# Partial sums of the down products parked in HBM, a ring of five places for second tiles, and two more units of seven products

## The chip, the core and the metric

The kernel runs on one core of a Trainium2 chip. TensorE (PE) multiplies, VectorE (DVE) and ScalarE (ACT) work elementwise, GpSimd (POOL) and SyncE (SP) are used here to issue DMA transfers. Each engine takes its instructions from a queue of its own, in order; an instruction that waits holds up all that stand behind it. The metric is the device time of one execution in microseconds (us).

## The reference

One encoder layer on 256 tokens of width 2048, in float32: a mixing sub-layer (attention and a recurrent block, `w_in`, `w_out`), a SwiGLU channel sub-layer with an inner width of 5632, and a per-layer embedding. The change lies in the middle one and its seams:

```python
h = h + rms_norm(mixed, g_mix_post[i])
fn = rms_norm(h, g_ffn_pre[i])
ff = (jax.nn.silu(fn @ w_ffn_gate[i]) * (fn @ w_ffn_up[i])) @ w_ffn_down[i]
h = h + rms_norm(ff, g_ffn_post[i])
gate = jax.nn.sigmoid(rms_norm(h, g_ple_pre[i]) @ w_ple_gate[i])
ple = p[i] @ w_ple_proj[i]
h = h + rms_norm(gate * ple, g_ple_post[i])
```

## The kernel before

**Products.** Every float32 operand is split in two parts of a narrower type: a cast on ScalarE gives the high part (`wh`, L614), a subtraction on VectorE the low part (`wl`, L627). A product is three matmuls, high x high, low x high, high x low (L661 to L663 in `products`, L672 to L674 in `product`). A weight tile is 256 rows by 512 columns, 512 KB, loaded by SyncE (L522 in the channel sub-layer, L539 elsewhere) into one of four places `wr` or a fifth, `third`. It serves 2 blocks of rows x 2 halves of the tokens x 3 = 12 matmuls of 512 columns.

**The channel sub-layer** goes in three parts of the inner width, `PARTS`: column chunks f = 0 to 3, 4 to 7, 8 to 10 of 512. In each part a group multiplies the gate and up tiles of one f in turns; their product goes to `mid`, is transposed (L333, and 16 small transfers `mT<-mid`, L343, on POOL and SyncE) and split again. Then two groups multiply the part with `w_ffn_down`, output chunks 0 and 1, and 2 and 3. The sums over the parts stand in `mg`: part 0 is copied there by ScalarE (L1778), part 1 added by VectorE (L1781), part 2 added in `Sub.chunk` (L1466), which also squares and multiplies with the gain (L1478).

**Units of seven.** Two tiles of the same rows (gate and up, or two down chunks), two blocks of rows and two halves of the tokens are a 2 x 2 x 2 product of blocks, eight products. A unit does it in seven, 21 matmuls instead of 24, with sums of blocks. `SEVEN_KS` names the blocks of rows treated so in the gate and up groups from f = 2 on (three units each), `DOWN_KS` those of the down groups of parts 0 and 1 (two units each). The host exchanges halves of the two tiles for it. For a unit, `sum_stream` adds weights on VectorE (L562, L566, L572), a third block comes from HBM by a transfer that adds to what is there (`added`, L583, POOL's queue). The unit then has a segment of four products in the group before its own (`four_products`), one of two (`two_products`) and a share in one of one (`one_product`); `made_of_four` combines the sums in PSUM. `issue` mixes these segments with the ordinary tiles of the group, by the tables `TAKEN` and `SPREAD`. The needed differences of activations are made by `sums_of`, `third_sums` (for `hF`) and `mid_sums` (for `mid`).

**Places.** The second tile R of a unit is held from its load until the split for its two products. It has three places, one for each number of the unit in its group: two in `lower`, which lies where the first half of the residual `h` was, and one in a half of `ple`. `h` and the other half of `ple` are written to HBM for the time of the channel sub-layer (`spill_h`, `spill_half`), and come back near its end (`reload_h`, L1596; `reload_half`, L1614). `pTh` and `pTl`, the split embedding input, are overwritten by the third sums, so `load_pT` (L1410) loads and splits `pT` a second time. The gain's tile serves as a fifth place for split weights until the last unit is through; then the gain `g_ffn_post` is loaded (L1422).

**The order** on the queues is decided when the program is built, by the class `Plan`: each piece of work is a generator that asks for an engine, a cost and perhaps a place; the planner starts whatever can start soonest by its own costs, and instructions are put on the queues in that order. `plan.add(work, ready, late)` hands it a piece with the time before which it isn't to start and a bonus or handicap. So a load that is handed over at `plan.clk["pe"]` is issued as soon as SyncE reaches it.

Of the kernel before, what the change touches and what calls it, by code (L numbers as in the profile page):

```python
# [39 lines left out]
DOWN_KS = (0, 2)  # L40
# [6 lines left out]
        (lambda c: (("w_ffn_down", c), ("w_ffn_down", c + 1)), (0, 2), [4 * f0 + k for k in DOWN_KS])  # L47
        for f0, _ in SEVEN_PARTS
# [186 lines left out]
def layer(ctx: ExitStack, tc: tile.TileContext, a: dict, out: bass.AP):  # L235
# [5 lines left out]
    plan = Plan(wr=R_BUFS, w=W_BUFS, sm=SM_BUFS, acc=4, ev=1, mid=2, bt=2, m2=1, mt=1, sq=1, T0=1, T1=1, T4=1, **{f"{s}{j}": n for s, m, n in (("p", 3, 1), ("t", 3, 0)) for j in range(m)}, wr0=1, w0=1)  # L241
# [188 lines left out]
    class Group:  # L430
# [23 lines left out]
        def two(self, j):  # L454
# [3 lines left out]
            lower[self.own[j] + 1] = j  # L458
# [13 lines left out]
        def issue(self, nxt):  # L472
# [7 lines left out]
            more = [lambda j=j: self.two(j) for j in range(len(self.sevens))]  # L480
            if self.sevens:
                more += [lambda js=js: self.one(js) for js in (range(2), range(2, len(self.sevens))) if js]
            for i, k in enumerate(self.rest[:m]):
                for j in range(len(nxt.sevens) if nxt else 0):
                    if i == n - 1 - (SPREAD if n > 5 and len(nxt.sevens) < 3 else 1) * (len(nxt.sevens) - 1 - j):
                        nxt.four(j)
# [3 lines left out]
                for _ in range(TAKEN.get((len(self.sevens), n), ())[i : i + 1][0] if more else 0):  # L490
                    more.pop(0)()
# [3 lines left out]
    SPREAD = 2  # L495
    TAKEN = {(2, 6): (1, 1, 1), (3, 5): (2, 3), (2, 4): (1, 2)}
# [14 lines left out]
    def load_stream():  # L511
        for i, tl in enumerate(tiles):
# [104 lines left out]
    def lo_stream():  # L617
        last_one = max(f[1] for f in fours.values())
        for i in range(len(tiles)):
# [12 lines left out]
            if i == half_end:  # L632
                plan.add(reload_half(), plan.now, -SOON)
# [99 lines left out]
    def two_products(group, j, i):  # L733
# [43 lines left out]
    def third_sums():  # L777
        for e in ev_embedded:
            yield e
        hi, lo = pT_pair()  # L780
        yield from sums_of(hF, 4, *(x.rearrange("p k s -> p (k s)") for x in (hi, lo)))
# [4 lines left out]

    def free_w(i):
# [1358 lines left out]
```

## Time and profile before

| | us |
|---|---|
| median of 3 runs | 1164.94 (1162.43 to 1167.70) |
| the profiled execution, its span | 1163.89, 1162.1 |
| TensorE busy in it | 1148.7 |
| VectorE, ScalarE busy | 883.0, 703.0 |
| bytes read from HBM, written | 242.57 MB, 5.24 MB |

A row of a group of instructions has line, engine, operation, what it writes and reads, count, then busy time and mean duration. A row of the order of time has start, duration, instruction, and in brackets the idle time before it and what ended it. "SPq" is SyncE's queue. `x222` behind a busy time is the number of instructions in the stretch. The channel sub-layer runs from about 350 to 1060 us: the down products of part 0 up to 620, those of part 1 up to 870, those of part 2 from about 988 to 1055.

### The profile page before, as it was taken

How to read it: one execution, taken by the hardware profiler on the slowest of the kernel's cores; microseconds unless marked ns; L12 is line 12 of the kernel's file. 1: busy time of each engine (PE TensorE's matmuls, PEld its weight loads, DVE VectorE, ACT ScalarE, POOL GpSimd, SP SyncE). 2: the span in 40 equal slices, each digit the busy share in tenths (PEclk: the TensorE clock that was granted, in tenths of full speed). 3: DMA queues.
4: the chain of work that ended last, by engine and by line, in shares of the span. 5: the costliest groups of instructions: out<-in, count | busy, mean ns of one | idle time of the engine just before them, and what ended most of it. 6: DMA issues, size and time to landing. Idle time of an engine off the chain costs nothing.

```text
span 1162.1 us, 15025 instructions
## 1 busy us (share of the span) xinstructions
PE 1148.7 (99%) x5225; PEld 951.3 (82%) x5225; DVE 883.0 (76%) x1096; ACT 703.0 (60%) x933; POOL 120.9 (10%) x198
## 2 busy tenths in 40 slices
PE   9999999999999999999999999999999999999997
PEld 7888888888888888788888888888888887887786
DVE  6678787888468777988778888887778884668575
ACT  6777777875456655655546556565455554456564
POOL 0000000000000123031000223312000311100000
PEclk9999999999999999999999999999999999999999
DMA  9867566546676887876775777877667668854772
GB/s 315 288 188 222 185 181 206 175 149 211 228 272 197 291 256 226 261 215 203 252 224 190 249 224 205 263 239 216 207 208 252 205 216 291 249 190 161 216 248 77
DMA packets 109964, 257.21 MB, mean 221 GB/s; under 512 B 38976, under 2 KB 46144, under 8 KB 108736
## 3 DMA queue, kind: packets, MB, share of 16 engines
q1 hardware_dynamic: 99552, 241.73, 62.5%
q0 software_dynamic: 9904, 14.17, 7.4%
q8 instruction: 41, 0.67, 0.2%
q10 hardware_dynamic: 432, 0.35, 0.1%
q14 instruction: 35, 0.29, 0.1%
HBM read 242.57 MB, written 5.24 MB: 213 GB/s over the span
## 4 chain that ended last, share of the span: by engine, by line
PE 86%; DMA 5%; DVE 4%; ACT 2%; issue 1%; POOL 1%; SPq 0%; ACTq 0%; DVEq 0%; POOLq 0%
PE acc L663 23%; PE acc L662 23%; PE acc L661 23%; PE acc L674 4%; PE acc L673 4%; PE acc L672 4%; DMA mT<-mid 3%; DVE wl L627 1%; POOL mT L343 1%; PE tr L324 1%; ACT wh L614 1%; DMA wr<-in_w_ple_gate 1%; DMA pw<-in_pT 1%; PE warm L2055 0%; PE pg L355 0%
## 5 line engine op out<-in xcount | busy, mean ns | idle before, releaser
L627 DVE TENSOR_TENSOR wl<-wr,wh 128x1024 fp32r<-128x1024 f32 (+1 forms) x313 | 373.9, 1209 | 131.7 <-ACT wh L614 129.7
L614 ACT CAST wh<-wr 128x1024 fp32r<-128x1024 f32 (+1 forms) x313 | 323.8, 1043 | 212.0 <-PE acc L662 142.0
L661 PE MATMUL acc<-wh,hT_mix_hi 128*128 128x512 f32 x420 | 164.4, 391 | 2.6 <-ACT wh L614 2.6
L662 PE MATMUL acc<-wh,hT_mix_lo 128*128 128x512 f32 x420 | 164.1, 391 | 0.3 <-DVE hT_mix_lo L313 0.3
L663 PE MATMUL acc<-wl,hT_mix_hi 128*128 128x512 f32 x420 | 164.2, 391 | 0.1
L343 POOL DMA_DIRECT2D mT<-mid x152 | 88.5, 589 | 570.0 <-DMA wr<-in_w_ffn_up 401.9
L663 PE MATMUL acc<-wl,hT_hi 128*128 128x512 f32 x320 | 124.9, 391 | 0.0
L661 PE MATMUL acc<-wh,hT_hi 128*128 128x512 f32 x316 | 124.4, 394 | 0.0
L662 PE MATMUL acc<-wh,hT_lo 128*128 128x512 f32 x316 | 123.1, 390 | 0.0
L661 PEld LDWEIGHTS acc<-wh,hT_mix_hi 128*128 128x128 f32 x420 | 79.2, 189 | 19.3 <-ACT wh L614 3.0
L614 ACT CAST wh<-ple 128x1024 fp32r<-128x1024 f32 (+1 forms) x52 | 51.8, 995 | 70.6 <-DVE ple L566 26.5
L663 PEld LDWEIGHTS acc<-wl,hT_mix_hi 128*128 128x128 f32 x420 | 79.1, 188 | 17.5 <-DVE wl L627 1.3
L662 PEld LDWEIGHTS acc<-wh,hT_mix_lo 128*128 128x128 f32 x420 | 79.2, 189 | 17.3 <-DVE hT_mix_lo L313 1.0
L663 PEld LDWEIGHTS acc<-wl,hT_hi 128*128 128x128 f32 x320 | 60.1, 188 | 13.6 <-DVE wl L627 0.9
L627 DVE TENSOR_TENSOR wl<-ple,wh 128x1024 fp32r<-128x1024 f32 (+1 forms) x52 | 59.6, 1150 | 13.7 <-ACT wh L614 13.1
L662 PEld LDWEIGHTS acc<-wh,hT_lo 128*128 128x128 f32 x316 | 59.4, 188 | 11.7
L661 PEld LDWEIGHTS acc<-wh,hT_hi 128*128 128x128 f32 x316 | 59.4, 188 | 11.3
L583 POOL DMA_DIRECT2D ple<-in_w_ffn_up x27 | 24.0, 887 | 245.1 <-DVE wl L627 164.7
L627 DVE TENSOR_TENSOR w<-wr,w 128x1024 fp32r<-128x1024 f32 x29 | 35.4, 1220 | 10.3 <-ACT w L614 9.7
L614 ACT CAST w<-wr 128x1024 fp32r<-128x1024 f32 x29 | 30.5, 1052 | 19.7 <-PE acc L662 14.5
L627 DVE TENSOR_TENSOR wl<-third,wh 128x1024 fp32r<-128x1024 f32 x29 | 35.4, 1221 | 8.6 <-ACT wh L614 7.7
L661 PE MATMUL acc<-wh,hT_ffn_hi 128*128 128x512 f32 x104 | 40.9, 393 | 0.6 <-ACT hT_ffn_hi L311 0.6
(429 smaller groups left out, 2389.9 us busy)
## 6 DMA issues: line engine op xcount, KB each, us to landing
wr<-in_w_in SPq DMA_DIRECT2D x77, 512.0 KB, 4.6
wr<-in_w_ffn_gate SPq DMA_DIRECT2D x70, 512.0 KB, 5.3
wr<-in_w_ffn_down SPq DMA_DIRECT2D x70, 512.0 KB, 4.7
wr<-in_w_ffn_up SPq DMA_DIRECT2D x55, 512.0 KB, 5.7
wr<-in_w_out SPq DMA_DIRECT2D x32, 512.0 KB, 4.0
wr<-in_w_ple_gate SPq DMA_DIRECT2D x32, 512.0 KB, 4.5
lower<-in_w_ffn_up SPq DMA_DIRECT2D x18, 512.0 KB, 5.0
third<-in_w_ffn_gate SPq DMA_DIRECT2D x18, 512.0 KB, 5.9
```

The source lines that it names most:

```text
L324: nc.tensor.transpose(tr[:, b, t * P : (t + 1) * P], e[:, t, sl], ident)
L343: (nc.gpsimd if i in pool else nc.sync).dma_start(dst[32 * j : 32 * j + 32, :, :, i, :], src[32 * i : 32 * i + 32, :, :, j, :],)
L583: nc.gpsimd.dma_start(dst, src, accum_op=ALU.add)
L614: nc.scalar.copy(his[i][:, 0 : src.shape[1], :] if n == 2 else his[i][:, j, :], src)
L627: nc.vector.tensor_tensor(out=los[i][:, m, :], in0=src, in1=f32(his[i][:, m, :]), op=ALU.subtract)
L661: nc.tensor.matmul(accs[t], hi[:, sl], his[i][:, j, :], start=st, stop=False, **group)
L662: nc.tensor.matmul(accs[t], lo[:, sl], his[i][:, j, :], start=False, stop=False, **group)
L663: nc.tensor.matmul(accs[t], hi[:, sl], los[i][:, j, :], start=False, stop=sp, **group)
L672: nc.tensor.matmul(dst, x[0], wh, start=start, stop=False, skip_group_check=seeded)
L673: nc.tensor.matmul(dst, x[1], wh, start=False, stop=False, skip_group_check=seeded)
L674: nc.tensor.matmul(dst, x[0], wl, start=False, stop=stop, skip_group_check=seeded)
```

## The change

**What it does.** The down products' sums of parts 0 and 1 are no longer held in `mg`. ScalarE copies each chunk to a `mid` tile and SyncE stores it to HBM (`parts`). When the last unit's two products are done, `reload_sums` brings part 0 back into `mg` by plain loads and adds part 1 by transfers on POOL's queue. The room of `mg` is used in between: one half as two more places for second tiles (`lower2`), the other for sums of activations (`s`). Second tiles take the five places in turn (`RING`). With `s`, the third sums no longer overwrite `pTh` and `pTl`, and `load_pT` goes. `DOWN_KS` gives the second down group of parts 0 and 1 a third unit. `FOURS` is a table of where the segments of four stand, and differs from the rule before for the first group of units and for groups of five ordinary steps before a group of two units. The reloads at the end get times of their own after the last unit: sums at 9, 13, 28 and 33, the gain at 37, `h` at 50 and 62, the half of `ple` at 76 us by the planner's clock.

```diff
+RING = 5
-DOWN_KS = (0, 2)
+DOWN_KS = {0: (0, 2), 2: (0, 2, 4)}
...
     def lower_tile(j):
-        if "lower" not in t2:
-            t2["lower"] = t2["pool"].tile([P, 2, 2, N], F32, tag="h0", name="lower")
         if j == 2:
             return t2["ple"][:, 1, 0 : D // 2].rearrange("p (k n) -> p k n", k=2)
-        return t2["lower"][:, j, :, :]
+        n, tag = ("lower", "h0") if j < 2 else ("lower2", "mg0")
+        if n not in t2:
+            t2[n] = t2["pool"].tile([P, 2, 2, N], F32, tag=tag, name=n)
+        return t2[n][:, j % 3, :, :]
...
-    SPREAD = 2
-    TAKEN = {(2, 6): (1, 1, 1), (3, 5): (2, 3), (2, 4): (1, 2)}
+    TAKEN = {(3, 5): (0, 2, 3), (2, 6): (0, 1, 1, 1)}
+    FOURS = {(8, 3): (3, 5, 7), (5, 3): (2, 3, 4), (6, 3): (3, 4, 5), (5, 2): (2, 4), (6, 2): (3, 5)}
...
-                    yield ev_half_spilled if lower[i] == 2 else ev_spilled
+                    yield (ev_spilled, ev_half_spilled, ev_unmerged)[(0, 0, 1, 2, 2)[lower[i]]]
...
             if i == half_end:
-                plan.add(reload_half(), plan.now, -SOON)
+                plan.add(reload_half(), plan.now + 76.0)
...
         if i == last_two:
-            plan.add(reload_h(), plan.clk["pe"], -SOON)
-        if i == last_third:
-            plan.add(load_pT(), plan.clk["pe"], -SOON)
+            for t in range(NT):
+                plan.add(reload_sums(0, t), plan.clk["pe"] + 9.0 + 4.0 * t)
+                plan.add(reload_sums(1, t), plan.clk["pe"] + 28.0 + 5.0 * t)
+                plan.add(reload_h(t), plan.clk["pe"] + 50.0 + 12.0 * t)
...
-            plan.add(next_gain(("ffn", "g_ffn_post"), plan.clk["pe"]), plan.clk["pe"])
+            plan.add(next_gain(("ffn", "g_ffn_post"), plan.clk["pe"] + 37.0), plan.clk["pe"] + 37.0)
...
-    pT = [Act(2) for _ in range(2)]
+    pT = [Act(2)] * 2
...
         def chunk(self, c, ch, add=False):
             sl = slice(c * N, (c + 1) * N)
+            if add:
+                yield ev_sums_back
...
     def down_post(part, c):
         def post(ch):
+            e = None
             for t in range(NT):
-                if part == 0:
-                    yield act(N)
-                    nc.scalar.copy(mg[:, t, sl], ch.accs[t])
-                else:
-                    yield dve(N)
-                    nc.vector.tensor_tensor(
-                        out=mg[:, t, sl], in0=ch.accs[t], in1=mg[:, t, sl], op=ALU.add
-                    )
+                yield act(N, take=None if t else "mid")
+                if not t:
+                    e = mid_tile()
+                nc.scalar.copy(e[:, t, :], ch.accs[t])
             ch.release()
+            yield dma(512)
+            nc.sync.dma_start(
+                parts[part].rearrange("t p d -> p t d")[:, :, c * N : (c + 1) * N], e
+            )
...
+    def reload_sums(part, t):
...
+        if part:
+            there = Event()
+            yield from added(t2["mg"].tiles[t], parts[part][t], there)
+            yield there
+            if t == NT - 1:
+                done(ev_sums_back)
+        else:
+            yield dma(1024)
+            nc.sync.dma_start(t2["mg"].tiles[t], parts[0][t])
...
+    for n, i in enumerate(sorted(lower)):
+        lower[i] = (3, 4, 0, 1, 2)[n % RING]
```

`sums_of` for the third blocks of `hF` writes to `s` now (`more_sums`), and `mid_sums` runs for the second block of a part too (rows 4 and 5), which the third unit of the second down group needs.

**Where instructions move.** Line numbers after the change are somewhat higher. First, ScalarE's queue where the last gate and up group runs. `wh<-wr` are casts of weights, `mid2h` casts of the transposed products, `pTh<-pw` that of the second load of `pT`. Before:

```order
L614 CAST wh<-ple 128x512
L614 CAST wh<-wr 128x1024 x4
L305 CAST mid2h_7734<-mT 128x512 x2
L614 CAST wh<-wr 128x1024
L305 CAST pTh<-pw 128x512
L614 CAST wh<-wr 128x1024 x3
L1695 ACTIVATE mid<-acc_7774,rstd_f 128x512
```

Now:

```order
L624 CAST wh<-ple 128x512
L624 CAST wh<-wr 128x1024 x3
L307 CAST mid2h_7783<-mT 128x512
L624 CAST wh<-wr 128x1024
L307 CAST mid2h_7783<-mT 128x512
L624 CAST wh<-wr 128x1024 x4
L1712 ACTIVATE mid<-acc_7826,rstd_f 128x512
```

The cast of `pTh` is gone, and one of the two casts of `mid2h` stands behind a cast of weights.

At the same place, SyncE's queue: `ple<-ple_spill`, the gain and `h<-h_spill` are reloads of 1 MB each, `mg<-part` those of part 0's sums. Before:

```order
L522 DMA wr<-in_w_ffn_up 128x1024
L1614 DMA ple<-ple_spill 128x2x1024
L1422 DMA gain_g_ffn_post<-in_g_ffn_post 128x2048
L1596 DMA h_8087<-h_spill 128x2048
L522 DMA wr<-in_w_ffn_gate 128x1024
L522 DMA wr<-in_w_ffn_up 128x1024
L522 DMA wr<-in_w_ffn_down 128x1024
L1596 DMA h_8088<-h_spill 128x2048
L522 DMA wr<-in_w_ffn_down 128x1024
L1410 DMA pw<-in_pT 128x2x256
L522 DMA wr<-in_w_ffn_down 128x1024 x4
L343 DMA mT<-mid 32x8x32 x8
```

Now:

```order
L532 DMA wr<-in_w_ffn_up 128x1024
L532 DMA wr<-in_w_ffn_down 128x1024 x3
L1827 DMA mg_8134<-part_98 128x2048
L532 DMA wr<-in_w_ffn_down 128x1024 x2
L1827 DMA mg_8135<-part_98 128x2048
L532 DMA wr<-in_w_ffn_down 128x1024 x2
L345 DMA mT<-mid 32x8x32 x8
L532 DMA wr<-in_w_ffn_down 128x1024 x4
L1424 DMA gain_g_ffn_post<-in_g_ffn_post 128x2048
L532 DMA wr<-in_w_ffn_down 128x1024 x7
L1610 DMA h_8136<-h_spill 128x2048
L532 DMA wr<-in_w_ffn_down 128x1024 x5
```

The four reloads of 1 MB and `pT` gave way to two of the sums, and the gain and `h` stand among the later weights.

Second, SyncE's queue where the first two groups of units are loaded (f = 2 and 3). A row `lower` or `ple` after a row `wr<-in_w_ffn_gate` is the second tile of a unit. Before, from the third unit of f = 2 to the first of f = 3:

```order
L522 DMA wr<-in_w_ffn_gate 128x1024
L522 DMA ple<-in_w_ffn_up 128x1024
L522 DMA wr<-in_w_ffn_gate 128x1024
L522 DMA wr<-in_w_ffn_up 128x1024
L522 DMA third<-in_w_ffn_gate 128x1024
L522 DMA wr<-in_w_ffn_up 128x1024
L522 DMA wr<-in_w_ffn_gate 128x1024
L522 DMA wr<-in_w_ffn_up 128x1024
L522 DMA wr<-in_w_ffn_gate 128x1024
L522 DMA lower<-in_w_ffn_up 128x1024
```

Now, the same stretch:

```order
L532 DMA wr<-in_w_ffn_gate 128x1024
L532 DMA lower<-in_w_ffn_up 128x1024
L532 DMA wr<-in_w_ffn_gate 128x1024
L532 DMA wr<-in_w_ffn_up 128x1024
L532 DMA wr<-in_w_ffn_gate 128x1024
L532 DMA third<-in_w_ffn_up 128x1024
L532 DMA wr<-in_w_ffn_gate 128x1024
L532 DMA wr<-in_w_ffn_up 128x1024
L532 DMA wr<-in_w_ffn_gate 128x1024
L532 DMA lower<-in_w_ffn_up 128x1024
```

Before, the last row goes to place 0, which the first unit of f = 2 holds; now it goes to place 1, which no unit has held yet.

Third, the end of POOL's queue, where `x24` are pieces of the last two transposed products. Before:

```order
L583 DMA ple<-in_w_ffn_up 128x512 x6
L343 DMA mT<-mid 32x8x32 x16
L583 DMA ple<-in_w_ffn_up 128x512 x3
L343 DMA mT<-mid 32x8x32 x24
L2142 UNCONDITIONAL_BRANCH
```

Now:

```order
L593 DMA ple<-in_w_ffn_up 128x512 x3
L345 DMA mT<-mid 32x8x32 x24
L593 DMA mg_8134<-part_101 128x2048
L593 DMA mg_8135<-part_101 128x2048
L2185 UNCONDITIONAL_BRANCH
```

The two transfers that add part 1's sums stand behind all pieces of the last product.

More of the change, by code (lines that the diff above doesn't have):

```diff
@@ L1441, in load_p2 @@
         pT[0].pair(0)
+    ev_sums_back = Event()
     class Sub:
@@ L1581, in layer @@
     ).tile([NT, P, D], F32, name="h_spill")
+    parts = [
+        ctx.enter_context(
+            tc.tile_pool(name=f"parts{i}", bufs=1, space=bass.MemoryType.DRAM)
+        ).tile([NT, P, D], F32, name=f"part{i}")
+        for i in range(2)
+    ]
     ev_spilled, ev_back = Event(), Event()
@@ L1590, in spill_h, with reload_h @@
         done(ev_spilled)
-    def reload_h():
-        t2["h"] = Halves(t2["pool"], "h")
-        for t in range(NT):
-            yield dma(1024)
-            nc.sync.dma_start(t2["h"].tiles[t], spill[t])
-        done(ev_back)
+    halves_back = []
+    def reload_h(t):
+        if "back" not in t2:
+            t2["back"] = Halves(t2["pool"], "h")
+        yield dma(1024)
+        nc.sync.dma_start(t2["back"].tiles[t], spill[t])
+        halves_back.append(t)
+        if len(halves_back) == NT:
+            t2["h"] = t2["back"]
+            done(ev_back)
     half_spill = ctx.enter_context(
@@ L1726, in carried @@
     def carried(mid, kk0, mT):
-        summed = kk0 == 0 and mid.ev_sums
+        summed = any(kk0 <= kx < kk0 + 4 for kx in mid.ev_sums)
         for b in range(0, 4, 2):
@@ L1831, in layer @@
                 ],
-                mid, ks, DOWN_KS if PARTS[part] in SEVEN_PARTS else (), apart=2 if end else 0,
+                mid, ks, DOWN_KS[c] if PARTS[part] in SEVEN_PARTS else (), apart=2 if end else 0,
                 after=load_sqrt if end else None,
```

98 lines of the change are left out of this document (53 added, 45 removed).

## The prediction

> **What bounds the kernel now.** I read the page's first part, then the table of stretches, then the chain of waits, then the queues at the places that the chain names.
>
> ```profile
> PE 1148.7 (99%) x5225; PEld 951.3 (82%) x5225; DVE 883.0 (76%) x1096; ACT 703.0 (60%) x933; POOL 120.9 (10%) x198
> ```
>
> TensorE is busy all the time: only fewer matmuls, or fewer moments in which it starves, can shorten this run. Where it starves, the stretches of 50 us show (first PE's busy time and its matmuls, then PEld, DVE, ACT, POOL; at the end granted clock, DMA share, GB/s):
>
> ```profile
> 400.00:450.00 50.00, 49.70 (x219) 40.51 (x218) 39.04 (x45) 27.79 (x32) 12.06 (x19) 1.00 0.83 251
> 450.00:500.00 50.00, 48.90 (x216) 40.15 (x215) 43.59 (x47) 27.91 (x31) 16.83 (x28) 1.00 0.79 239
> 550.00:600.00 50.00, 50.00 (x222) 41.40 (x221) 35.98 (x36) 27.79 (x30) 2.61 (x3) 1.00 0.75 239
> 700.00:750.00 50.00, 49.87 (x219) 40.63 (x218) 44.36 (x49) 28.91 (x32) 15.57 (x26) 1.00 0.76 232
> 950.00:1000.00 50.00, 47.38 (x202) 38.37 (x201) 29.78 (x29) 21.16 (x24) 13.91 (x24) 0.97 0.74 227
> ```
>
> An undisturbed stretch holds 222 matmuls of 512 columns, 50 / 222 = 0.225 us each. Against it the others lack 3, 6, 3 and 20 matmuls: 0.7, 1.35, 0.7 and 4.5 us. These four losses are all that the channel sub-layer leaves to gain beside the matmuls themselves. The largest, in the chain of waits:
>
> ```profile
> 976.03 7.87 DMA pw<-in_pT
> 983.89 0.02 issue
> 983.92 0.04 ACT pTh L305
> ...
> 984.44 1.05 ACT wh L614
> 985.49 0.04 issue
> 985.53 0.80 PE acc L661
> 986.33 0.43 PE acc L662
> ```
>
> The second load of `pT` takes 7.87 us to land, ScalarE's cast of it (L305) waits, the cast of a weight tile (L614) stands behind it, and TensorE waits for that. ScalarE and SyncE at this place, in order of time:
>
> ```profile
> 977.00 1.05 ACT L614 CAST wh<-wr 128x1024 fp32r<-128x1024 f32 x1 [3.06 <-DMA wr<-in_w_ffn_gate]
> 983.92 0.62 ACT L305 CAST pTh<-pw 128x512 fp32r<-128x512 f32 x1 [5.87 <-DMA pw<-in_pT]
> 984.44 2.93 ACT L614 CAST wh<-wr 128x1024 fp32r<-128x1024 f32 x3
> ```
>
> ```profile
> 959.98 0.60 SPq L1614 DMA_DIRECT2D ple<-ple_spill  x1
> 963.26 0.33 SPq L1422 DMA_DIRECT2D gain_g_ffn_post<-in_g_ffn_post  x1
> 963.64 1.09 SPq L1596 DMA_DIRECT2D h<-h_spill  x1
> ...
> 971.20 0.43 SPq L1596 DMA_DIRECT2D h<-h_spill  x1
> ```
>
> Three casts of weights run the moment `pTh` is done, so their tiles were there already: ScalarE stood idle 5.87 us for a tile that is needed only at the very end of the stage. Four transfers of 1 MB within 12 us are why it came late.
>
> The loss of 1.35 us has another cause. SyncE's queue, then VectorE's:
>
> ```profile
> 441.91 0.33 SPq L522 DMA_DIRECT2D wr<-in_w_ffn_gate  x1
> 452.97 0.33 SPq L522 DMA_DIRECT2D lower<-in_w_ffn_up  x1
> ...
> 456.38 0.44 SPq L522 DMA_DIRECT2D wr<-in_w_ffn_gate  x1
> ```
>
> ```profile
> 451.76 1.18 DVE L627 TENSOR_TENSOR wl<-lower,wh 128x1024 fp32r<-128x1024 f32 x1
> ...
> 464.93 0.69 DVE L562 TENSOR_TENSOR ple<-wr 128x512 f32<-128x512 f32 x1 [3.77 <-DMA wr<-in_w_ffn_gate]
> ...
> 468.38 1.22 DVE L627 TENSOR_TENSOR wl<-wr,wh 128x1024 fp32r<-128x1024 f32 x1
> ```
>
> SyncE issues nothing for 11 us: its next load goes to place 0 of `lower`, whose holder is split only at 451.76. Then six loads go out in 4 us, VectorE waits 3.77 us for one of them, and TensorE stops for the splits behind it.
>
> **The change, part by part.** *Two more units of seven.* Each takes 21 matmuls instead of 24: 6 matmuls, 6 x 0.225 = 1.35 us off TensorE. Their price elsewhere, per unit, from these rows:
>
> ```profile
> L562 DVE TENSOR_TENSOR ple<-wr 128x512 f32<-128x512 f32 x31 | 21.2, 685 | 6.9 <-DMA wr<-in_w_ffn_gate 6.9
> L627 DVE TENSOR_TENSOR wl<-ple,wh 128x1024 fp32r<-128x1024 f32 (+1 forms) x52 | 59.6, 1150 | 13.7 <-ACT wh L614 13.1
> ```
>
> Three sums of weights (3 x 0.685) and one and a half further splits (1.5 x 1.15), 3.8 us of VectorE; casts on ScalarE of about the same length as the splits, 1.7 us; an accumulating load of 256 KB. The differences of the activations come once more in each part: four of 128 columns, at half the 512-column time at most, and a split, 4 x 0.34 + 0.69 = 2.0 us. Some 11 us of VectorE over the two parts, against idle time of 14 us in the one stretch 550 to 600 above: I cost it at nothing. Without that cover it would cost up to 11 us.
>
> *The sums parked.* Part 0's copies stay on ScalarE (to `mid` instead of `mg`); part 1's move to it from VectorE:
>
> ```profile
> L1778 ACT COPY mg<-acc x8: 580/587/588, 570.8 to 618.5; 128x512 f32<-128x512 f32 x8
> L1781 DVE TENSOR_TENSOR mg<-acc,mg x8: 679/681/682, 822.5 to 870.3; 128x512 f32<-128x512 f32 x8
> ```
>
> VectorE loses 8 x 0.68 = 5.4 us, ScalarE gains 8 x 0.587 = 4.7 us; both are idle enough there. Eight stores of 512 KB stand on SyncE, each behind two copies, and the weight loads stand behind them. SyncE already spends its time waiting for room (`422.5` us in the row below), so 2.3 us for four copies cost nothing unless the copies are late; bounds 0 and 2.3, I take 0. The place in `mid` is asked for next by a gate product one whole group later, 16 tiles of 12 matmuls or 43 us.
>
> ```profile
> SPq L522 <- DVE wl L627: 422.5, 161, 12.7
> ```
>
> *Five places.* The load that held SyncE for 11 us goes to a place never used before. I count the 1.35 us as gone, and the 0.7 us of the first stretch (three units in a row there, now spread over the group by `FOURS`). The loss at 700 to 750 has no cause that the change plainly removes: kept. Bounds 0 and 2.75, taken 2.0.
>
> *No second `pT`, and the reloads spread.* The cast at 983.92 goes, and nothing late stands before the weights: 4.5 us. Ends: 0 (another late tile holds ScalarE) and 4.5; I take 4.5, because the three tiles behind it had landed. The half of `ple`, the gain and the residual come later, each 1 MB:
>
> ```profile
> gain_g_ple_post<-in_g_ple_post SPq DMA_DIRECT2D x1, 1024.0 KB, 4.8
> h<-h_spill SPq DMA_DIRECT2D x2, 1024.0 KB, 11.4
> mT<-mid SPq DMA_DIRECT2D x56, 32.0 KB, 2.5
> ple<-in_w_ffn_up POOLq DMA_DIRECT2D x27, 256.0 KB, 4.6
> ```
>
> 4.8 us alone, 11.4 in a crowd. The gain, the soonest wanted, stands on SyncE's queue after 11 of the 24 weight tiles of the last down products and is read after the first 12 were used; with four tiles or more of lead on SyncE that is some 5 x 2.7 = 13 us: nothing on the path.
>
> *The sums come back.* This is the new cost. Part 0's come by two plain loads where the old reloads stood. Part 1's are added by two transfers of 1 MB on POOL's queue, which stand behind the last block's pieces; their user is the first addition on VectorE:
>
> ```profile
> 994.69 3.45 POOL L343 DMA_DIRECT2D mT<-mid  x6 [0.52 <-issue]
> ```
>
> ```profile
> 1018.39 1.22 DVE L627 TENSOR_TENSOR wl<-wr,wh 128x1024 fp32r<-128x1024 f32 x1 [1.50 <-ACT wh L614]
> 1019.57 1.37 DVE L1466 TENSOR_TENSOR mg<-acc,mg 128x512 f32<-128x512 f32 x2
> ...
> 1025.71 4.78 DVE L627 TENSOR_TENSOR wl<-wr,wh 128x1024 fp32r<-128x1024 f32 x4
> ```
>
> POOL is free at 998.1; the additions begin at 1019.6 and 1020.3, so there are 21 to 22 us. No transfer of 1 MB that adds is in this trace. Low end: as a plain one, 4.8 us each, 11 us early. High end: four times the 256 KB row, 4 x 4.6 one after the other, 37 us. Between them: 4.6 less 2.5 (the 32 KB row, nearly all fixed time) is 2.1 us for 224 KB, 9.3 us for 992 KB; two on the same engines land 2.5 + 18.6 us after an issue at about 999 to 1000, at 1021. That is 0.8 us late. Behind the additions wait the splits; the next one, at 1025.71, is 4.6 us later than the steady 2.72 us would have it and TensorE missed nothing. The tile it makes is wanted four tiles after the cast, about 1028.6, so some 1.7 us more are free. On the middle value nothing is lost, on worse ones several: I put 1.0 us down.
>
> *Sum.* 1.35 + 4.5 + 2.0 - 1.0 = 6.85 us off the profiled execution of 1163.89 us (span 1162.1): 1157.0 us. The median of the runs stands 1.05 us above that execution, 1164.94: I predict 1158.1 us, 0.59% less.
>
> The Trainium skill, "DMA: Bandwidth & Descriptors", section "Anatomy of one DMA — SWDGE (gpsimd) path", gives a transfer from this queue 2.0 us and its bytes at 436 GB/s: as an estimate 2.6 us for 256 KB, where the row has 4.6, and 4.4 us for 1 MB. By it the sums would be back well in time and the sum 7.85 us, 1157.1 us; the row speaks against the page for transfers that add.
>
> The same skill, "TensorE: Matmul & The Clock Gate", section "What's actually happening", lets the clock fall to half only after an idle window of about 3.4 us. The chain shows matmuls of 0.43 us after an idle time of under 3 us (983 to 985.5) and a granted clock of 0.97: here the shorter gap was enough, the loss 4.5 us and not the idle time alone. By the page's window about 1.75 us less would be won, 1159.9 us.
>
> **The rivals.** *B, all four losses go and the sums are in time:* 1.35 + 7.25 = 8.6 us less, 1156.3 us. For it: fewer loads bunch up on SyncE everywhere. Against: VectorE is at 44.36 of 50 in the stretch 700 to 750, and that load stays.
>
> *C, the sums return late and TensorE stops once:* the weights' loads share the 16 DMA engines with them (share 0.74 before). Three us beyond the slack and slow matmuls after it, as at 985.5 (4.5 lost for 2.75 idle, so 1.75 more), instead of my 1.0: 1157.1 + 4.75 = 1161.9 us.
>
> *D, the stall at 983 stays:* the two plain loads of the sums now stand where the spills stood, and the last blocks' `mT` come late as well; the 4.5 us are not won: 1162.6 us. Against it: ScalarE waited for `pT`, not for a weight.
>
> *E, slower:* the two adding transfers go one after the other at the high end, 37 us. They land at 1036, VectorE's queue stands for 15.5 us at the first addition, 13.8 beyond the slack, and with the slow matmuls TensorE loses 15.5: 1172.6 us. It turns the sign when TensorE stops for more than 6.9 us. For it: one queue carries both. Against: nothing in the trace shows such transfers one at a time.
>
> That the change does not do what it says is excluded for the matmuls, whose count falls by 6.
>
> **How the numbers follow.** The forecast has 0.46, with its own range 1156.5 to 1160.5 (the three runs of before spread over 5.3 us); B 0.16; C 0.18; D 0.08; E and whatever else holds a queue for over 10 us 0.12. Half a per cent, 5.8 us, is about what a measurement of this kernel tells from no change: faster means under 1159.1, slower over 1170.8. Of the forecast 0.36 lies below 1159.1 and 0.10 above; with B that makes faster 0.52, with C and D same 0.36, with E slower 0.12. The range leaves E out and takes in C and D and B's lower edge: 1155 to 1164.
>
> **What would show it.** Right: 6 matmuls fewer; no cast of `pTh` in the second half; 222 matmuls in every 50 us from 950 on; no gap of 11 us between weight loads on SyncE near 450; the additions on VectorE near 1012 (1019.6 less the 7.85 us gained until then) start without waiting for a DMA. Wrong: a wait of VectorE for the transfers `mg<-part` with TensorE's count falling behind it (C, E), a weight cast waiting behind `mid2h` near 975 (D), or new waits of TensorE for `wl` in the down products, where VectorE has the added sums.

## The result and the profile after

The changed kernel takes 1165.12 us, median of 22 runs (1161.28 to 1168.26), against 1164.99 us for the kernel before, also 22 runs (1161.61 to 1169.27): ratio 1.0001, 95% interval 0.9991 to 1.0011. The two can't be told apart. The forecast of 1158.1 us was 7.0 us too low. The profiled execution took 1162.47 us (span 1160.7) where the working had come to 1157.0 us.

The engines of the changed kernel (busy time, share of the span, instructions):

```profile
PE 1146.8 (99%) x5219; PEld 951.5 (82%) x5219; DVE 887.0 (76%) x1107; ACT 710.5 (61%) x946; POOL 124.7 (11%) x202
```

Six matmuls fewer, as the change says. VectorE has 4.0 us more and ScalarE 7.5 us more, which are the additional sums, splits and copies. The stretches of 50 us, columns as before:

```profile
400.00:450.00 50.00, 49.27 (x217) 40.26 (x216) 38.79 (x45) 27.14 (x31) 12.37 (x19) 1.00 0.86 272
450.00:500.00 50.00, 50.00 (x223) 41.40 (x222) 45.59 (x54) 29.36 (x33) 18.16 (x30) 1.00 0.72 216
700.00:750.00 50.00, 50.00 (x223) 41.40 (x221) 46.49 (x54) 28.90 (x33) 18.15 (x30) 1.00 0.72 217
950.00:1000.00 50.00, 50.00 (x222) 41.41 (x221) 30.58 (x29) 22.83 (x25) 15.79 (x26) 1.00 0.72 211
1000.00:1050.00 50.00, 46.74 (x195) 37.29 (x194) 25.94 (x27) 22.90 (x31) 0.00 (x0) 0.97 0.91 310
```

Three of the four old losses are gone: 450 to 500, 700 to 750 and 950 to 1000 hold 222 or 223 matmuls. The first stretch is no better than before (217, then 219), and a new one, 1000 to 1050, holds 195: 27 fewer than it could, with the DMA engines busy for 0.91 of the time (0.69 in the same stretch before). Its chain of waits:

```profile
994.92 1.05 ACT wh L624
995.97 0.02 issue
995.99 1.24 DVE wl L637
997.23 0.02 issue
997.25 17.06 DMA wr<-in_w_ffn_down
1014.31 0.02 issue
...
1014.41 1.05 ACT wh L624
1015.46 0.02 issue
1015.48 1.23 DVE wl L637
1016.72 0.04 issue
1016.76 0.50 PE acc L673
```

One load of a weight tile of 512 KB, the most ordinary transfer of this kernel, takes 17.06 us instead of about 5. SyncE's and POOL's queues around it:

```profile
990.37 2.53 SPq L532 DMA_DIRECT2D wr<-in_w_ffn_down  x4
992.96 0.66 SPq L1424 DMA_DIRECT2D gain_g_ffn_post<-in_g_ffn_post  x1
997.25 2.16 SPq L532 DMA_DIRECT2D wr<-in_w_ffn_down  x2
```

```profile
990.87 1.89 POOL L593 DMA_DIRECT2D mg<-part  x2
```

POOL issues both adding transfers at once, at 990.9. They land at 1002.9 and 1009.1, in 12.0 and 17.7 us. ScalarE's idle times show who pays:

```profile
1003.14 1.05 ACT L624 CAST wh<-wr 128x1024 fp32r<-128x1024 f32 x1 [5.35 <-DMA wr<-in_w_ffn_down]
1009.42 1.04 ACT L624 CAST wh<-wr 128x1024 fp32r<-128x1024 f32 x1 [5.23 <-DMA wr<-in_w_ffn_down]
```

The user of the sums pays nothing. VectorE comes to its first addition ten us after they landed, and waits for no DMA (without TensorE's stops ahead of it, of 5.96 us in all, it would have come some 4 us after they landed, an estimate):

```profile
1019.14 1.28 DVE L1472 TENSOR_TENSOR mg<-acc,mg 128x512 f32<-128x512 f32 x2
```

To compare executions I add up, from the trace, how far the starts of neighbouring matmuls lie apart beyond the usual 0.227 us. This is TensorE's loss, in us, in the places where it exceeds 0.35 in a run (a dash: it does not; left out are the losses at 351, 1060 and 1152, which all kernels share, and one near 1095, in the last sub-layer, which comes and goes between 0 and 1.9 us). The last two columns are the ratio to the kernel before and its interval.

| kernel | 426-436 | 466-472 | 717-723 | 982-992 | 995-1031 | ratio | 95% |
|---|---|---|---|---|---|---|---|
| before | 0.84 | 1.38 | 0.69 | 4.61 | - | 1 | |
| before, again (e7) | 0.60 | 1.77 | 1.20 | 6.21 | - | | |
| changed | 1.18 | - | - | - | 5.96 | 1.0001 | 0.9991 to 1.0011 |
| e1 gain early | 5.58 | - | - | - | 2.69 | 1.0007 | 0.9994 to 1.0020 |
| e2 sums early | 4.63 | - | - | - | 4.99 | 0.9984 | 0.9964 to 1.0005 |
| e3 plain loads | 4.59 | - | - | - | - | 0.9969 | 0.9955 to 0.9984 |
| e4 no part 1 | 4.42 | - | - | - | - | 0.9972 | 0.9959 to 0.9985 |
| e5 sums of units later | 0.46 | - | - | - | 5.31 | 0.9978 | 0.9968 to 0.9988 |
| e6 adds apart | 3.44 | - | - | - | 4.13 | 0.9999 | 0.9985 to 1.0013 |
| e8 as e5, three places | 0.88 | 2.57 | 1.27 | - | 5.47 | 0.9997 | 0.9983 to 1.0011 |
| e9 before, pT late | 0.95 | 1.53 | 0.93 | - | - | 0.9954 | 0.9940 to 0.9968 |
| c1 VectorE adds | 4.97 | - | - | - | 1.67 | 0.9974 | 0.9961 to 0.9987 |
| c2 = c1 + e5 | 1.12 | - | - | - | 1.45 | 0.9938 | 0.9916 to 0.9959 |
| c3 = c2, later adds | 0.82 | - | - | - | - | 0.9927 | 0.9909 to 0.9945 |

The second column tells more than the profile of the changed kernel alone. Up to 950 us e1 to e4, e6 and c1 have the same instructions in the same order as the changed kernel, so they are six more executions of that part: they lose 3.4 to 5.6 us at 426 to 436, where the changed kernel's own profile happened to lose 1.18.

### The profile page after: what moved, and what is told of

It reads as the page before. It is cut to its first block, busy times and chain, and to the rows that moved or that the text cites. A ratio compares the mean times of both kernels' runs of the same rounds, so it can differ in the third digit from the quotient of the medians.

```text
span 1160.7 us, 15071 instructions
## 1 busy us (share of the span) xinstructions
PE 1146.8 (99%) x5219; PEld 951.5 (82%) x5219; DVE 887.0 (76%) x1107; ACT 710.5 (61%) x946; POOL 124.7 (11%) x202
## 4 chain that ended last, share of the span: by engine, by line
PE 88%; DMA 5%; DVE 3%; ACT 2%; issue 1%; POOL 1%; SPq 0%; ACTq 0%; DVEq 0%; POOLq 0%
PE acc L673 23%; PE acc L672 23%; PE acc L671 23%; PE acc L684 5%; PE acc L682 5%; PE acc L683 5%; DMA mT<-mid 2%; DMA wr<-in_w_ffn_down 1%; DMA wr<-in_w_ple_gate 1%; DVE wl L637 1%; ACT wh L624 1%; PE tr L326 1%; POOL mT L345 1%; PE warm L2098 0%; PE pg L357 0%
## 5 line engine op out<-in xcount | busy, mean ns | idle before, releaser
L672 PE MATMUL acc<-wh,hT_mix_lo 128*128 128x512 f32 x400 | 155.9, 390 | 0.3 <-DVE hT_mix_lo L315 0.3
L671 PE MATMUL acc<-wh,hT_mix_hi 128*128 128x512 f32 x400 | 156.0, 390 | 0.0
L673 PE MATMUL acc<-wl,hT_mix_hi 128*128 128x512 f32 x400 | 155.7, 389 | 0.0
L672 PEld LDWEIGHTS acc<-wh,hT_mix_lo 128*128 128x128 f32 x400 | 75.1, 188 | 16.4 <-DVE hT_mix_lo L315 1.0
L671 PEld LDWEIGHTS acc<-wh,hT_mix_hi 128*128 128x128 f32 x400 | 75.1, 188 | 15.5
L673 PEld LDWEIGHTS acc<-wl,hT_mix_hi 128*128 128x128 f32 x400 | 75.1, 188 | 15.5
L672 PEld LDWEIGHTS acc<-wh,hT_lo 128*128 128x128 f32 x316 | 59.4, 188 | 11.5
L671 PEld LDWEIGHTS acc<-wh,hT_hi 128*128 128x128 f32 x316 | 59.5, 188 | 11.4
L593 POOL DMA_DIRECT2D ple<-in_w_ffn_up x27 | 24.0, 891 | 234.7 <-DVE wl L637 195.9
L672 PE MATMUL acc<-wh,hT_ffn_lo 128*128 128x512 f32 x104 | 40.8, 393 | 0.5 <-DVE hT_ffn_lo L315 0.5
L673 PE MATMUL acc<-wl,hT_ffn_hi 128*128 128x512 f32 x104 | 40.5, 390 | 0.0
L671 PE MATMUL acc<-wh,mid2h 128*128 128x512 f32 x96 | 38.3, 399 | 2.2 <-ACT wh L624 2.2
```

The costliest lines, as they stand in the source:

```text
L593: nc.gpsimd.dma_start(dst, src, accum_op=ALU.add)
L671: nc.tensor.matmul(accs[t], hi[:, sl], his[i][:, j, :], start=st, stop=False, **group)
L672: nc.tensor.matmul(accs[t], lo[:, sl], his[i][:, j, :], start=False, stop=False, **group)
L673: nc.tensor.matmul(accs[t], hi[:, sl], los[i][:, j, :], start=False, stop=sp, **group)
```

## The experiments

**What holds the loads back at 1000.** Three theories: T1, transfers that add are dear by themselves; T2, it is the third megabyte, the gain, that tips it; T3, neither, but the order of work on ScalarE and POOL.

*e1: the gain's load alone back to its old place, about 30 us earlier.*

```
-plan.add(next_gain(("ffn", "g_ffn_post"), plan.clk["pe"] + 37.0), plan.clk["pe"] + 37.0)
+plan.add(next_gain(("ffn", "g_ffn_post"), plan.clk["pe"] + 0.0), plan.clk["pe"] + 0.0)
```

> The changed kernel loses 5.96 us of TensorE between 1009 and 1021 us (summed over neighbouring matmuls: how far their starts lie apart beyond the usual 0.227 us), while five loads of 512 KB for the down products take 11.4 to 17.1 us to land, beside two adding transfers of 1 MB (issued together at 990.9, landed at 1002.9 and 1009.1) and the 1 MB of the gain (issued at 992.96, landed at 1013.0). Here the gain alone goes back to where it stood before, about 30 us earlier; all else is the changed kernel's. Theory T1, the adding transfers by themselves keep the weights' loads back: those loads still take over 10 us, the loss stays at 4.5 us or more, time within 1.5 us of the changed kernel's (ratio to before 0.999 to 1.001). Theory T2, the third megabyte among them decides: the loads take under 9 us, the loss is under 1.5 us, the time 4.5 us shorter (ratio 0.995 to 0.997). Theory T3, neither (the order of ScalarE's and POOL's work): loss unchanged with loads under 9 us.

The gain's load is issued at 966.4. The loads beside the adding transfers still take 12.1 to 17.3 us; the loss is 2.69 instead of 5.96 us, but the time is not shorter (1.0007). T2 as stated falls, and T1's bound of 4.5 us is missed too. Whether the gain has a share in the loss isn't shown: e6 below, whose instructions up to 1020 us stand in the same order, lost 4.13.

*e2: the sums come back earlier.*

```
-plan.add(reload_sums(0, t), plan.clk["pe"] + 9.0 + 4.0 * t)
-plan.add(reload_sums(1, t), plan.clk["pe"] + 28.0 + 5.0 * t)
+plan.add(reload_sums(0, t), plan.clk["pe"] + 1.0 + 2.0 * t)
+plan.add(reload_sums(1, t), plan.clk["pe"] + 12.0 + 5.0 * t)
```

> The parked sums come back sooner: the plain loads of part 0 about 8 us and the adding transfers about 16 us earlier than in the changed kernel, ahead of the last block's eight pieces on POOL's queue; the gain stays where the changed kernel has it. T1: the adding transfers still spread 12 to 18 us over the weights' loads, so the loss of 4 to 6 us only moves, to about 995 to 1005, and the last block's pieces come late on top (they stand behind 2 MB on the same queue): ratio to before 1.000 to 1.004. T2: without the gain beside them the loads take under 9 us, the gain's own 1 MB lands in about 5 us, the loss is under 1.5 us, ratio 0.995 to 0.997. T3: loss at 1009 to 1021 unchanged.

Each adding transfer now waits for the plain load of part 0 that it adds to (landed at 972.5 and 988.4), so they run one after the other, from 973.1 and 988.9, and still take 13.0 and 11.3 us; four loads of weights beside the first take 11.5 to 14.4 us, and the second of those plain loads, of 1 MB, 14.5. The gain, far from both, landed in 8.8 us. The losses are 0.80 us at 995 and 4.19 at 1006. The second is not simply the old loss at another place, as T1 has it: beside the second adding transfer the 16 pieces of the last block took 3.9 to 7.2 us to land (1.9 to 3.7 in the changed kernel), and the last landed at 1005.29. ScalarE's casts of the block came at 1005.85, ahead of casts of weights, and SyncE, where eight of the pieces stand, issued no weights from 992 to 1002. The time itself is spread widely, 1157.89 to 1166.37 us, and the profiled execution was the slowest of the ten; the ratio, 0.9984, cannot be told from 1 (T1 expected 1.000 to 1.004).

*e3: the same two transfers without the addition* (part 0's sums are thereby missing from the output).

```
-            yield from added(t2["mg"].tiles[t], parts[part][t], there)
...
+            nc.gpsimd.dma_start(t2["mg"].tiles[t], parts[part][t])
...
```

> The two transfers of part 1's sums are plain loads on the same queue at the same places, without the addition (so part 0's sums are left out of the output; all else is computed). The same bytes are read. T1, it is the adding that takes the engines' time: each of the two lands in under 8 us, the weights' loads beside them take under 9 us, the gain under 10 us, the loss falls below 1.5 us, ratio to before 0.995 to 0.997. T2, it is 3 MB of reloads within 2 us beside 0.5 MB each 2.7 us, however written: the loads still take over 10 us, the loss stays above 4 us, ratio 0.999 to 1.001. T3: no change in the loss with loads under 9 us.

TensorE loses nothing after 960, and the time falls to 1160.19 us. The order on every queue is the changed kernel's. The two transfers land in 7.95 and 11.15 us. The DMA engines from 993 to 1009 us, by queue (q0 is POOL's; packets, MB, share of 16 engines), first the changed kernel, then this one:

```profile
q0 software_dynamic: 290, 2.10, 63.3%
q1 hardware_dynamic: 568, 2.21, 38.8%
```

```profile
q1 hardware_dynamic: 1394, 3.72, 62.4%
q0 software_dynamic: 369, 2.17, 36.0%
```

For about the same 2.1 MB the packets of the adding form take 0.633 x 16 = 10.1 us of the 16 engines, those of the plain one 5.8. Together 4.31 MB pass in these 16 us with the addition and 5.89 without, with the engines nearly full both times. That is T1, with a correction: the loads still took up to 11.1 us here, not under 9 as expected, and TensorE missed nothing at that.

*e4: neither transfer* (part 1's sums are missing from the output).

```
-            yield from added(t2["mg"].tiles[t], parts[part][t], there)
+            done(there)
             yield there
```

> The two adding transfers are left out (part 1's sums are missing from the output); part 0's loads, the gain and all else stay in place. This prices the return of part 1's sums by itself. T1 and T2: the loads beside the gain take 5 to 8 us, the loss at 1009 to 1021 is under 0.5 us, and the time falls by the full 6 us: 1158.5 to 1160 us, ratio 0.994 to 0.996. T3, the order of ScalarE's and POOL's work: the loss stays above 4 us, ratio 0.999 to 1.001.

No loss after 960; 1160.78 us, 0.9972. The gain lands in 8.5 us. That is less than the 6 us expected: the two transfers are worth 0.29% of the time, 3.4 us, with some 1.9 us either way by the two intervals (an estimate). Why it is less than the 5.96 us of the profile stays open; e5 and e8 below lose 5.31 and 5.47 us at the same place, so that profile was no exception. T3 is out: ScalarE's and POOL's order is unchanged in e3.

*e6: the second adding transfer 11 us behind the first, with the gain early.*

```
-plan.add(reload_sums(1, t), plan.clk["pe"] + 28.0 + 5.0 * t)
+plan.add(reload_sums(1, t), plan.clk["pe"] + 28.0 + 16.0 * t)
```

> The gain goes back to where it stood before, as in the earlier run where TensorE lost 2.69 us at 1013 to 1016; in addition the second adding transfer of 1 MB is issued about 11 us later, after the first has landed. T1, an adding transfer holds the DMA engines 5 to 6 us per MB and what hurts is that two of them run together: each now lands within 9 us of its issue, weights' loads beside them take under 10 us, and the loss between 1000 and 1020 is under 0.7 us. Rival, the total of the bytes in these 30 us is too much wherever they are put: loads still take over 12 us, loss stays between 2 and 6 us. Rival with the other sign, the second now lands too late for the first addition: VectorE waits for it, loss over 3 us. In time, with the loss between 426 and 434 unchanged: ratio to before 0.996 to 0.998 by T1, 0.999 to 1.001 by the first rival.

It did not do what it was meant to: POOL issued them at 992.3 and 992.9. The number moves the transfer in the plan, but POOL has nothing else to do and no semaphore to wait for, so only the order counts, and that stayed. It is e1 once more (loss 4.13, ratio 0.9999). Only e2 has the two transfers apart, at an earlier place and at a cost of its own; behind the last block's pieces that was not tried.

*c1: VectorE adds.* Part 1's sums come by plain loads into the residual's two places, whose reload follows; all is computed.

```
-            yield from added(t2["mg"].tiles[t], parts[part][t], there)
+                t2["more"] = Halves(t2["pool"], "h")
...
+            nc.sync.dma_start(t2["more"].tiles[t], parts[1][t])
...
+            for c in range(4):
+                yield dve(N)
+                sl = slice(c * N, (c + 1) * N)
+                nc.vector.tensor_tensor(
+                    out=t2["mg"].tiles[t][:, sl], in0=t2["mg"].tiles[t][:, sl],
+                    in1=t2["more"].tiles[t][:, sl], op=ALU.add,
+                )
```

> Nothing is added by a transfer: part 1's sums come by two plain loads of 1 MB on SyncE's queue into the two places of the residual (which comes back behind them), and VectorE adds them in eight additions of 128x512 (8 x 0.68 = 5.4 us). All is computed. T1, the cost is that of adding transfers: the loads land within 12 us, TensorE loses under 1 us between 1005 and 1025, ratio to before 0.996 to 0.998, as in the run with plain loads (0.9969). Rival, VectorE's 5.4 us or its wait for these loads (it holds the weights' splits behind it) costs as much as was won: VectorE waits for the sums, loss of 2 to 6 us between 1000 and 1020, ratio 0.999 to 1.002.

0.9974, as T1 expected, but the loss is 1.67 us, between the two expectations. VectorE waits 5.18 us for the load of its first such addition, as the rival says, and the split behind that addition is late:

```profile
1004.86 0.69 DVE L1830 TENSOR_TENSOR mg<-mg,h 128x512 f32<-128x512 f32 x1 [5.18 <-DMA h<-part]
1005.47 1.22 DVE L637 TENSOR_TENSOR wl<-wr,wh 128x1024 fp32r<-128x1024 f32 x1
```

**What is lost at 430.** The six executions show it better than the changed kernel's own profile. The chain of e1 there:

```profile
405.36 9.06 DMA mT<-mid
...
414.71 0.47 POOL mT L345
415.19 0.10 issue
415.28 0.58 POOL mT L345
415.86 0.86 POOL ple L593
416.73 0.34 issue
417.06 8.10 DMA mT<-mid
425.16 0.02 issue
425.18 0.63 ACT mid0h L307
...
428.98 0.41 DVE mT L1766
429.39 1.15 DVE wl L637
430.54 0.04 issue
430.58 0.80 PE acc L684
431.38 0.43 PE acc L682
```

POOL issues the 16 pieces of the block and stops again and again for the landing of earlier ones: its transfers use eight semaphores in turn, so each waits until the one eight before it has landed (the piece at 414.71 for that of 405.36). Ahead of the last two pieces stands an adding load (L593, `ple`) of the first unit of seven. The last piece lands at 425.2, and the block's split, its differences (L1766) and the weights' split follow on VectorE. The adding load stands there because `FOURS` lets the first unit's sums begin after tile 3 instead of 5.

*e5: this one row back.*

```
-    FOURS = {(8, 3): (3, 5, 7), ...
+    FOURS = {(8, 3): (5, 6, 7), ...
```

> In four executions of kernels that share the changed kernel's program up to 950 us, TensorE loses 4.4, 4.6, 4.6 and 5.6 us between 426 and 434; the changed kernel's own profile shows 1.18 there, the kernel before 0.84 at 434 and 1.38 at 468. Here one row of FOURS goes back to what the kernel before did: in the first group (8 weight tiles deep, feeding 3 units) the sums of the three units start after tiles 5, 6 and 7, not 3, 5 and 7; so no adding load stands on POOL's queue among the last pieces of the first block. All else is the changed kernel's. Theory L1, that adding load and its wait hold up the last two pieces, and the splits of the block stand behind them on VectorE: the loss between 426 and 434 falls under 1 us, and the time by 3 to 4.5 us against the changed kernel (ratio to before 0.996 to 0.998). L2, the loads that the five places let ahead crowd the 16 DMA engines there: the loss stays above 3 us, ratio 0.999 to 1.001. Beside it a loss as of before (0.8 to 1.4) may come back near 468 under L1.

The loss is 0.46 as L1 expects, the ratio 0.9978, 2.7 us below the changed kernel's (3 to 4.5 were expected). POOL's queue has the pieces without the load between:

```profile
402.82 5.99 POOL L345 DMA_DIRECT2D mT<-mid  x10 [401.06 <-DMA wr<-in_w_ffn_gate]
410.24 2.91 POOL L345 DMA_DIRECT2D mT<-mid  x5 [1.44 <-DMA mT<-mid]
413.99 0.58 POOL L345 DMA_DIRECT2D mT<-mid  x1 [0.84 <-DMA mT<-mid]
418.73 0.97 POOL L593 DMA_DIRECT2D ple<-in_w_ffn_up  x1 [4.16 <-DVE w L637]
```

That the row costs the time is shown. L2 as stated, the five places by themselves, falls: they are all still there. What in the row costs it was not separated, and the place of the adding load on POOL's queue can't be all. The changed kernel's own profile has the same order, its slowest piece took 6.8 us to land, and it lost 1.18; in the six executions that lost 3.4 to 5.6 the slowest piece took 7.8 to 9.1 us, and in e1 the slow ones were issued from 405 on, before the adding load. The row also draws other loads forward on SyncE: the second tiles of the first two units are issued at 396.2 and 409.8 in e1, at 407.0 and 415.2 in e5, and from 395 to 405 the engines move 337 and 281 GB/s. So transfers that crowd each other there remain a possible cause.

**What the parts are worth.**

*e7: the kernel before, unchanged.*

> The kernel before once more, for a second profiled execution. If its losses (0.84 us at 434, 1.38 at 468, 4.61 at 983 to 989) are the same to 0.5 us in each execution, they are what the change removes; if they vary by several us, as the changed kernel's between 426 and 434 do (1.2 to 5.6), one execution was too little to read them from.

The same four places, 0.2 to 1.6 us apart (9.78 us in all against 7.52). Half a microsecond was too narrow for 983. For this kernel one execution tells where the losses are, and their size to about 1.5 us; for the changed kernel's loss at 430 it did not (1.18 against 3.4 to 5.6).

*e8: e5 with three places.*

```
-RING = 5
+RING = 3
```

> The kernel with the sums after tiles 5, 6 and 7 (ratio 0.9978), with three places instead of five for the second tiles. It prices the five places. If they are what removed the stop near 468 (1.38 and 1.77 us in two executions of the kernel before): a gap of about 10 us between loads on SyncE comes back and a loss of 1 to 2 us between 440 and 480, ratio 0.9985 to 1.0. If they are worth nothing, the loss there stays under 0.3 us and the ratio is 0.997 to 0.9985.

SyncE's gap is back, and with it 2.57 us at 468 (1 to 2 expected) and 1.27 at 720; against e5 the time rises by 0.0019, 2.2 us, with some 2.0 either way by the two intervals (an estimate):

```profile
443.00 0.33 SPq L532 DMA_DIRECT2D wr<-in_w_ffn_gate  x1
454.08 0.33 SPq L532 DMA_DIRECT2D lower<-in_w_ffn_up  x1
```

So the five places do what the prediction held, and also cure the loss at 720, which it had kept.

*e9: the kernel before, with only the second load of `pT` put later.*

```
-            plan.add(load_pT(), plan.clk["pe"], -SOON)
+            plan.add(load_pT(), plan.clk["pe"] + 60.0, -SOON)
```

> The kernel before with one change: the second load of pT and its cast stand some 15 weight tiles later in SyncE's and ScalarE's queues; nothing else of the change is in it. The prediction held that this cast alone causes the stop at 983 (4.61 and 6.21 us in two executions). If so: the loss at 980 to 992 falls under 0.7 us, and the time by 4 to 5.5 us, ratio to before 0.995 to 0.997. If another late transfer of the crowd (four of 1 MB within 12 us) takes its place: the loss stays at 2 us or more, ratio 0.998 to 1.0.

```profile
950.00:1000.00 50.00, 50.00 (x222) 41.41 (x221) 32.18 (x32) 24.44 (x28) 13.90 (x24) 1.00 0.80 256
```

The load and its cast now stand at 1025.7 and 1031.1, and TensorE waits for neither. The stop at 983 is gone, and nothing took its place, though the four transfers of 1 MB stand where they did: 1158.61 us, ratio 0.9954, 5.4 us. This one number, without anything else of the change, is worth four fifths of the 6.85 us that the forecast expected of all of it.

**A version that beats both.** *c2 is c1 with e5's row:*

```
+    FOURS = {(8, 3): (5, 6, 7), ...
...
+            nc.sync.dma_start(t2["more"].tiles[t], parts[1][t])
```

> Both edits that paid alone, together: the sums of the first three units after tiles 5, 6 and 7 (alone: ratio 0.9978), and part 1's sums by plain loads and eight additions on VectorE (alone: 0.9974). If the two losses are separate, as their places 580 us apart say, they add: loss under 1 us near 430, 1.5 to 2 us near 1005 (VectorE's first such addition waits for its load), ratio 0.994 to 0.997, about 1158 us. If the gain is given back elsewhere (another wait later), ratio 0.997 to 0.998.

1157.49 us, 0.9938: the two gains add (alone 0.9974 and 0.9978). The 1.45 us at 1001 is the wait of c1.

*c3 puts the additions behind four more splits:*

```
+LAND = 8.0
...
             nc.sync.dma_start(t2["more"].tiles[t], parts[1][t])
+            plan.now += LAND
             done(here)
```

> As the run before it, but the eight additions stand on VectorE behind four more splits of weights, about 10 us later, so that the splits no longer wait behind the first addition for its load. T1: the loss of 1.7 us near 1005 falls below 0.5 us, ratio 0.993 to 0.996, about 1157 us. Rival: the additions now collide with the four additions of part 2 and the last products' splits, and a loss of 1 to 3 us appears between 1012 and 1030, ratio 0.995 to 0.998.

1156.19 us, ratio 0.9927 (0.9909 to 0.9945): of the table's losses only 0.82 us at 433 is left (1.9 at 1088 besides, in the last sub-layer). It can't be told from c2 (their intervals overlap); against e9, which changes one number of the kernel before, it is 2.4 us shorter, with some 2.7 either way (an estimate from the intervals).

```profile
950.00:1000.00 50.00, 50.00 (x222) 41.42 (x221) 30.96 (x30) 23.89 (x26) 13.90 (x24) 1.00 0.73 238
1000.00:1050.00 50.00, 50.00 (x223) 41.39 (x222) 35.23 (x44) 26.65 (x40) 0.00 (x0) 1.00 0.83 308
```

## Why the prediction was wrong

Step by step, by its own terms:

- *Six matmuls, 1.35 us:* right, 5219 matmuls. The cover for their price held: VectorE's busy time rose by 4.0 us (expected 11 less 5.4) in stretches that lost nothing.
- *No second `pT`, 4.5 us:* right, and the choice of the upper end too: 4.61 and 6.21 us were there, none is left, and e9 shows that the second load with its cast was the cause. Rival D fell.
- *The early losses, 2.0 us:* wrong. The five places work as described (e8), and even the 0.7 us kept for 700 to 750 went. But the working stopped at "now spread over the group by `FOURS`" and took the new places of the first group for a gain. Its row (8, 3) puts an adding load among the last pieces of the first block on POOL's queue and draws loads forward; the changed kernel's own profile lost 1.18 there, six other executions 3.4 to 5.6 us, and e5 takes it away (0.0023 of the time, 2.7 us). Of the 0.84 + 1.38 + 0.69 = 2.9 us before, these executions won nothing and lost 0.5 to 2.7.
- *The sums come back, 1.0 us:* this is the step that failed most. It asked when the two transfers land and who reads them, and its size for that was nearly right: 21.1 us from the issue for both, by its middle value, and 18.3 measured, issued at 990.9 because all ran earlier. No reader waited. But by the same value the two hold the 16 engines for 18.6 us, and the working let the weights' loads, one each 2.7 us, pay nothing for it. They paid: five loads of 512 KB took 11.4 to 17.1 us, the gain 20.1, and TensorE lost 5.96 us in the profiled execution. e3, with the same bytes in the same order and no addition, lost nothing. The rival C had this mechanism in a half sentence ("the weights' loads share the 16 DMA engines"), but hung it on the sums being late, which they were not. (Rival E's limit for the sign, 6.9 us, should by its own sum be 7.85.)
- *The reloads spread, nothing on the path:* right for the gain's reader: it landed at 1013.0, and VectorE read it at 1020.6 without waiting for it. Wrong in its working: the 11 weight tiles ahead of it on SyncE were out by 992.6, and it followed at 992.96, in the same 2 us as the adding transfers, into the crowd. No share of the time shows for it (e1, 1.0007).

For the profiled execution the sum closes nearly: 5.0 us more for the sums than the 1.0 put down, 0.3 for the early losses (2.91 less 1.18 is 1.73, not 2.0), of the 5.5 us by which it missed. The median missed by 7.0. By the ratios the two transfers cost 3.4 us (e4) where 1.0 was put down, and the row of `FOURS` 2.7 (e5) where nothing was: 5.1 of the 7.0. The rest lies within their intervals, some 1.9 and 1.6 us either way (estimates). That a usual execution of the changed kernel loses at 430 what the six others lost is argued from their equal order, not seen: it has one profile.

The Trainium skill, "DMA: Bandwidth & Descriptors", section "Anatomy of one DMA — SWDGE (gpsimd) path", with its 2.0 us and the bytes at 436 GB/s, gives 4.4 us for 1 MB, an estimate. The traces do not agree: 12.0 and 17.7 us adding, and 7.95 and 11.15 us plain beside the same loads. The prediction was right to go by its row.

What the prediction named as signs: the matmuls and `pT` came right, and SyncE's gap near 450 shrank to 7.6 us. "222 matmuls in every 50 us from 950 on" held to 1000 and failed behind it (195), and so told of the miss. The additions without a wait came right as well, and proved nothing: none of the signs for wrong names a slow load of weights beside the transfers, the one thing that happened.

## What to carry to other kernels

Price a transfer by the time that it holds the DMA engines, and look for its cost at whatever else is in flight, not only at its reader: here the reader waited for nothing and TensorE stopped for a weight tile. Where a sum comes back from HBM, a plain load and a few additions on an engine with idle time can be cheaper than a transfer that adds (c1, 0.9974 against 1.0001). Ask first what one part of a change would win by itself: e9 won 5.4 us with one number. A time in a plan moves nothing on an engine that has no wait there: check the order and the semaphores, and take a second execution before sizing a loss of a few us.

## What was unexpected of the hardware

By their packets' times, two transfers that add 1 MB each took the 16 engines for 1.75 times as long as the same bytes without the addition (10.1 against 5.8 us for 2.1 MB), and five loads of 512 KB from SyncE's queue beside them took 11.4 to 17.1 us.

TensorE's clock fell after stops well under 3 us, but not always: in e1 at 1013 the starts of two pairs of neighbouring matmuls lay 2.01 and 0.92 us apart, 0.34 us between the pairs, and the matmuls behind ran at 0.23 us (granted clock 1.00 from 1016 to 1020); in e6 at 1010 it was 1.89 and 0.93 us, and seven matmuls followed at 0.43 us (granted clock 0.57 from 1014 to 1018). The Trainium skill, "TensorE: Matmul & The Clock Gate", section "What's actually happening", has the clock halve after an idle window of about 3.4 us that runs free of the program. That like stops had different consequences agrees with a free-running window; that stops of together under 3 us were enough, with matmuls between them, does not agree with a whole idle window. Nor does the length of a stop give that of the slow stretch: behind 3.17 us in e7 at 982 ten matmuls ran at 0.43 us, behind 3.20 and then 1.18 us in e1 at 426 five.
